# Last feed-forward group of an encoder trunk in seven products, and two gate products side by side

## The chip, the cores and the metric

The kernel runs on 1 core of one Trainium2 chip. The time is device microseconds (us) of one execution of the whole program. The engines in the tables are PE (matmul; PEld is its weight load), DVE (vector), ACT (scalar, activation), POOL (here: the issuer of accumulating DMAs) and SP (the issuer of the other DMAs).

## What is computed

A trunk of two layers over 768 tokens (one request of 512, one of 256) with 1024 features, everything in float32. A layer is a token mixer (attention in layer 0, a short gated convolution in layer 1), a feed-forward block with 4096 hidden features, and a gated addition of a per-layer input `p`:

```python
for i in range(DEPTH):
    h = rms_norm(x, norm_mix[i])
    x = x + (window_attention(h, ...) if i % 2 == 0 else short_conv(h, ...))
    h = rms_norm(x, norm_mlp[i])
    x = x + jnp.square(jax.nn.relu(h @ mlp_w_up[i])) @ mlp_w_down[i]
    gate = jax.nn.sigmoid(rms_norm(x, norm_ple[i]) @ ple_w_gate[i])
    x = x + (p[i] @ ple_w_proj[i]) * gate
return rms_norm(x, final_norm)
```

The change touches the end of the feed-forward block and the start of the gate, in both layers.

## The kernel before

`x` lies transposed: 8 blocks of 128 features by 768 tokens. Every float32 matrix product is made of three products of split operands: high weight by high input, high by low, low by high. The high part is a rounded copy (ACT, "hi"), the low part is the source minus the high part (DVE, "lo", 128x1024 for one block of weights; or a DMA that adds the source onto the negated high part, issued by POOL: `added`, tiles `vlo`).

Most of the feed-forward block uses a scheme of seven products where four times two halves would take eight: the weights of two blocks are read as a 2x2 grid and give w11, w12, w22 and the sums s1 to s4; the inputs give x11, x21, x22 and the sums t1 to t4 (class `Acts`). `product7` is one such product, over half of the tokens (H = 384 columns), accumulated in a PSUM bank. ACT copies intermediate banks into other banks (`C` and `B` from `a`, `p` from `b`), and later products accumulate into the copies.

`mlp(l, ...)` runs 16 units `up` (each makes 128-row blocks of the hidden features; its results are `y1`, `y2`) and, for each group g of two units, `down` in two halves h (4 of the 8 blocks of `x` each, 14 products of 6 matmuls). The body stands in `manual_schedule`: on ACT, PE and DVE the instructions run in the order in which the code is written, and each engine takes them strictly in that order. In a half of `down` the order on PE is w11, s3, s2, w12, s1, w22, s4. Between them DVE adds the finished banks to `x` (lines 1341 and 1363) and, for the step after, prepares the weight sums (lines 419 to 425) and low parts (line 464); ACT makes the copies (1336, 1357) and the high parts (444).

The last group, g = 7, is different: `last_down` makes it with plain products (`group2`, line 131), 4 chunks of 48 matmuls of 384 columns. After each two blocks of `x`, `add` (line 869) brings the result into `x`, and `nxt.block` makes the high part (ACT, 188), the low part (DVE, 189) and the square (ACT 198, DVE 199) of that block for the norm ahead of the gates.

The gates follow: eight products of 48 matmuls, one for each block of gate columns (512-column and 256-column pieces of tokens apart in layer 1). `ple` is layer 0: after the first gate product come the four `ss` matmuls (the sum of squares) and the chain to `rstd` (the norm's factor); each gate then is multiplied with `rstd` (DVE, 1463), goes through the sigmoid (ACT, 1466), is multiplied with the projected `p` (1469) and added to `x` (1470), and the block is prepared for layer 1's mixer. Its products 0 to 5 are ordered by the framework, the others by hand. `last_ple` is layer 1: first all weights, then two gate products, then `rstd`.

Of the kernel before, what the change touches and what calls it, by code (L numbers as in the profile page):

```python
# [11 lines left out]
F32 = mybir.dt.float32  # L12
F32R = mybir.dt.float32r
# [5 lines left out]
P = 128  # L19
# [28 lines left out]
def trunk_kernel(ctx: ExitStack, tc: tile.TileContext, a: dict, out: bass.AP):  # L48
# [124 lines left out]
    class Norm:  # L173
# [4 lines left out]
        def __init__(self, i, name, places, acc, rstd=None):  # L178
            self.i, self.name, self.places, self.rplace = i, name, places, rstd
            self.xs = [], []  # L180
            self.acc = slot(acc, f"acc_{name}", F32)[:, : self.n]

        def block(self, m, xb):
            g = gain(self.i, m)
            hi, lo = (slot(self.places[8 * p + m], f"xs_{self.name}") for p in range(2))
            self.xs[0].append(hi[:])
            self.xs[1].append(lo[:])
            act.activation(hi[:], xb, AF.Copy, scale=g)
            dve.scalar_tensor_tensor(lo[:], xb, g, hi[:].bitcast(F32), ALU.mult, ALU.subtract)
            self.square(m, xb)  # L190
# [854 lines left out]
    def mlp(l, norm, nxt, w, places, early, product=None, begun=None):  # L1045
# [14 lines left out]
        def acts_of(u, y1, y2, rest):  # L1060

            own = places[7 * (u % 2) : 7 * (u % 2) + 7]
            e = Acts(y1, y2, own, groups[u // 2], u % 2)
            if u < 2 * NG - 2:
                return [
                    lambda: squared(rest),
                    lambda: e.highx(0),
                    lambda: (e.highx(1), e.lowx(0), e.lowx(1), e.t13()),
                    e.t42,
                    lambda: e.high(0),  # L1070
                    lambda: e.high(1),
                    lambda: e.low(0),
                    lambda: e.low(1),
                ]

            def whole(i, q):
                hi, lo = slot(own[2 * i], "act"), slot(own[2 * i + 1], "act")
                split(hi[:], lo[:], q[:])
                groups[u // 2].setdefault("whole", {})[u % 2, i] = hi[:], lo[:]

            return [lambda: squared(rest), lambda: whole(1, y2), lambda: whole(0, y1)]
# [22 lines left out]
        def up_begun(u, w, make, then):  # L1104
# [71 lines left out]
        def up_plain(u, w, make, then):  # L1176
# [91 lines left out]
        def up(u, w, make, then):  # L1268


            first = u == PLAIN[l]
# [35 lines left out]
            rectified(y1, c, 0, H, ALU.max)  # L1307
            late()
            if seven:
                v.low("direct")  # L1310
            else:
                v = [then(0)]
# [5 lines left out]
            squared(y2)  # L1318
            product7(a, w, "s4", xs, False)
            rectified(y1, a, H, T, ALU.max)  # L1320
            pend.extend(acts_of(u, y1, y2, y1))
            return v

        def down(g, h, w, make, then):

            xg = groups[g]
            top, low = ([x(4 * h + 2 * i + s) for s in range(2)] for i in range(2))
# [14 lines left out]

            w.low("s32")
# [9 lines left out]
            b = [bank("B", "b")[:, :H] for _ in range(2)]  # L1353
            products(b, "s3", True)
            p = big("p")
            for i in range(2):
                act.activation(p[:, i * H : i * H + H], b[i], AF.Copy)
            products(a, "s2", False)
            d = copies("B", a)
            for i in range(2):  # L1360
                t = low[i].rearrange("p (a n) -> p a n", a=2)
                q = p[:, None, i * H : i * H + H].broadcast_to([P, 2, H])
                dve.tensor_tensor(t, t, q, ALU.subtract)
# [15 lines left out]
        def last_down(chunks, then):  # L1379
            late(9)  # L1380
            src = [groups[NG - 1]["whole"][k] for k in ((0, 0), (1, 0), (0, 1), (1, 1))]
            for j in range(KB // 2):
                if j + 1 < KB // 2:
                    chunks.append(then(j + 1))
                ps = [both(), both()]
                ts = [terms_of(chunks[j], [[t[p] for t in src] for p in range(2)], col=i * P) for i in range(2)]

                for i, part in ((0, 0), (1, 0), (0, 1), (1, 1)) if j == 0 else ((0, None), (1, None)):
                    if part is None:
                        group2(ps[i], ts[i])  # L1390
                    else:
                        group2(ps[i], (ts[i][::2], ts[i][:0:-2])[part], part == 0, part == 1)
                    if part != 0:
                        m = 2 * j + i
                        add(m, ps[i])
                        nxt.block(m, x(m))
# [5 lines left out]
        for g in range(NG - 1):  # L1402
            jobs += [ups[2 * g + 2], (down, g, 0), (down, g, 1), ups[2 * g + 3]]
        with tc.manual_schedule(engines={ET.Activation, ET.PE, ET.DVE}):
            for i, (job, *args) in enumerate(jobs):

                def make():

                    if i + 1 == len(jobs):
                        return None  # L1410
                    what, *n = jobs[i + 1]
                    if what is not down:
                        return up_chunk(l, *n)
                    k = (KB // 2) * n[0] + 2 * n[1]
                    return Weights7(a_down[k], a_down[k + 1])

                a_down = a["down"][l]
                w = job(*args, w, make, lambda j: weight(a["down"][l, (NG - 1) * (KB // 2) + j], FG))
            last_down(w, lambda j: weight(a["down"][l, (NG - 1) * (KB // 2) + j], FG))
# [24 lines left out]
    def ple(norm, nxt):  # L1444
# [30 lines left out]
        for i in range(5):  # L1475
            gp = product(PAIRED[i], weights(i))
# [59 lines left out]
    def last_ple(norm, full, rest, prs, ys, finals):  # L1536

        rest = [[slot(rest[2 * p + i], "gwr") for i in range(2)] for p in range(2)]
        ws = []
        for m in range(KB):  # L1540
            if m < 2:
                w = weight(a["gate"][1, m], KB)
            else:
                raw, i = fetch(a["gate"][1, m]), m - 2
                most = [slot(full[6 * p + i], "gw")[:] for p in range(2)]
                less = [rest[p][i // 3][:, i % 3 * (CH - T) : (i % 3 + 1) * (CH - T)] for p in range(2)]
                split(*most, raw[:, :T])
                split(*less, raw[:, T:])
                w = tuple(blocks(most[p], T // P) + blocks(less[p], (CH - T) // P) for p in range(2))
            ws.append(w)  # L1550
# [9 lines left out]
        gps = [product(first, m) for m in range(2)]  # L1560
# [10 lines left out]
        outs = [more.tile([P, CH], F32, tag=tag, name="o", bufs=1) for tag in ("sum0", "sum1", "zhi", "zlo")]  # L1571
# [30 lines left out]
        def stored(n):  # L1602

            for _ in range(n):
                i = left.pop(0)
                o = outs[i // 2][:, i % 2 * s0 : i % 2 * s0 + s0]
# [282 lines left out]
    with tc.manual_schedule(engines={ET.Activation, ET.PE, ET.DVE}):  # L1889
        w0, *begun = first_tail(n1, act0[5:7] + act0[12:], *head)  # L1890
        mlp(0, n1, n2, w0, act0, KB // 2, begun=begun)
    n3 = Norm7(1, "mix1", xs3, aside3, rest[24], spare=dict(zip(("ah", "al", "v"), old[13:])))
    wc = ple(n2, n3)
# [4 lines left out]
    mlp(1, n4, n5, w1, act1, KB // 2, begun=begun)  # L1898
    last_ple(
        n5,  # L1900
        full=xs1[17:] + act1[:1],
        rest=act1[1:5],
        prs=act1[5:8],
        ys=act1[8:11],
        finals=((act1[11], act1[12]), (act1[13], xs1[16])),
# [79 lines left out]
```

## Time and profile before

| | before |
|---|---|
| median of 3 runs | 1660.08 us (1659.68 to 1662.16) |
| the profiled execution | 1661.51 us, its span 1659.5 us |
| mean granted clock of TensorE | 0.996 |
| busy PE / DVE / ACT / POOL | 1637.6 / 1380.8 / 948.5 / 71.7 us |
| layer 0: group 6's two halves, `last_down`, first gate begins | at 705.64, 749.77 and 783.15 us |
| layer 1: `last_down`, first gate begins | at 1543.07 and 1576.59 us |

A line of the timeline has the start (us), the duration of the first instruction to the last one of the row, the engine, the line of the program, the operation, output<-input tiles, shapes and the number of instructions; brackets hold the idle time ahead of it and what ended that. A window's line has the window's length, busy time and count of each engine, the granted clock, the DMA share and GB/s. A line of waits has the engine and instruction, what it waited for, the sum, how often, and the longest.

### The profile page before, as it was taken

What the parts mean: (1) busy time and instruction counts of PE and PEld (TensorE: products, weight loads), DVE (VectorE), ACT (ScalarE), POOL (GpSimd) and SP (SyncE); (2) the same over time, 40 slices, a digit from 0 to 9 for tenths busy, and PEclk for the clock granted to TensorE, in tenths of its full rate; (3) what the DMA queues carried; (4) which work ended last, traced back from release to release, by engine and by line L of the source; (5) the groups of instructions that cost most, each with busy time, mean ns of one, the idle gap of its engine ahead of it and who ended that gap; (6) DMA issues with size and microseconds to landing.
All of it is one profiled execution on the core that took longest, in us unless ns stands there. A gap on an engine that the chain in (4) does not pass through costs nothing.

```text
span 1659.5 us, 24297 instructions
## 1 busy us (share of the span) xinstructions
PE 1637.6 (99%) x9414; PEld 1587.3 (96%) x9414; DVE 1380.8 (83%) x2242; ACT 948.5 (57%) x1508; POOL 71.7 (4%) x104
## 2 busy tenths in 40 slices
PE   8999999999999999999999999999999999999997
PEld 7988789999999999999999999999999999999986
DVE  7598888898889889877888777778889888988776
ACT  7377766865556556545654434555555655655554
POOL 0211000000000000000000000000000000000000
PEclk9999999999999999999999999999999999999998
DMA  8755322443233333242312222112333323333222
GB/s 267 199 154 149 87 64 83 121 109 87 83 86 96 96 96 91 71 122 69 98 62 77 76 77 76 64 64 73 87 96 96 95 87 79 90 96 108 69 87 99
DMA packets 55476, 161.11 MB, mean 97 GB/s; under 512 B 7056, under 2 KB 10128, under 8 KB 55360
## 3 DMA queue, kind: packets, MB, share of 16 engines
q1 hardware_dynamic: 45184, 139.89, 26.4%
q0 software_dynamic: 10176, 19.67, 6.7%
q8 instruction: 74, 1.21, 0.3%
q14 instruction: 42, 0.34, 0.1%
HBM read 138.82 MB, written 10.48 MB: 90 GB/s over the span
## 4 chain that ended last, share of the span: by engine, by line
PE 88%; DVE 7%; ACT 4%; issue 1%; DMA 0%; DVEq 0%; SPq 0%; ACTq 0%
PE a L486 33%; PE mm L131 10%; PE mm L140 8%; PE b L486 8%; PE d L486 5%; PE c L486 5%; PE B L486 4%; PE C L486 4%; PE gate L140 3%; PE pt L760 1%; PE p L1096 1%; PE p L1199 1%; PE gate L131 1%; PE O L770 1%; PE O L771 1%
## 5 line engine op out<-in xcount | busy, mean ns | idle before, releaser
L486 PE MATMUL a<-xs,whi 128*128 128x384 f32 x624 | 121.8, 337 | 0.0
L444 ACT ACTIVATE vhi<-wraw 128x512 fp32r<-128x512 f32 x67 | 42.2, 631 | 132.3 <-PE B L486 87.9
L486 PEld LDWEIGHTS a<-xs,whi 128*128 128x128 f32 x624 | 110.0, 188 | 0.2 <-DVE y L1306 0.2
L486 PE MATMUL a<-t,zhi 128*128 128x384 f32 x536 | 109.1, 337 | 0.0
L486 PE MATMUL a<-t,whi 128*128 128x384 f32 x536 | 108.8, 336 | 0.0
L486 PE MATMUL b<-t,zhi 128*128 128x384 f32 x536 | 108.7, 336 | 0.0
L1341 DVE TENSOR_TENSOR x<-x,a 128x384 f32<-128x384 f32 x112 | 62.1, 554 | 55.3 <-PE a L486 55.3
L486 PE MATMUL a<-act,whi 128*128 128x384 f32 x448 | 96.5, 337 | 0.0
L486 PEld LDWEIGHTS a<-t,whi 128*128 128x128 f32 x536 | 94.9, 188 | 0.0
L486 PEld LDWEIGHTS b<-t,zhi 128*128 128x128 f32 x536 | 94.9, 188 | 0.0
L486 PEld LDWEIGHTS a<-t,zhi 128*128 128x128 f32 x536 | 94.8, 188 | 0.0
L464 DVE TENSOR_TENSOR wlo<-wraw,whi 128x1024 fp32r<-128x1024 f32 x70 | 85.2, 1218 | 7.9 <-ACT whi L444 7.9
L444 ACT ACTIVATE whi<-sum 128x1024 fp32r<-128x1024 f32 x67 | 70.6, 1054 | 27.0 <-PE a L486 22.7
L464 DVE TENSOR_TENSOR wlo<-sum,whi 128x1024 fp32r<-128x1024 f32 x67 | 81.8, 1220 | 5.1 <-ACT whi L444 5.1
L1058 ACT ACTIVATE y<-y 128x768 f32<-128x768 f32 x64 | 53.7, 839 | 54.4 <-DVE y L1055 54.3
L464 DVE TENSOR_TENSOR zlo<-sum,zhi 128x1024 fp32r<-128x1024 f32 x67 | 81.5, 1217 | 0.0
L140 PE MATMUL mm<-xs_mix,whi 128*128 128x512 f32 (+1 forms) x320 | 81.0, 341 | 0.0
L486 PEld LDWEIGHTS a<-act,whi 128*128 128x128 f32 x448 | 79.8, 188 | 0.0
L444 ACT ACTIVATE whi<-wraw 128x1024 fp32r<-128x1024 f32 x72 | 75.7, 1051 | 7.0 <-PE C L486 7.0
L444 ACT ACTIVATE zhi<-sum 128x1024 fp32r<-128x1024 f32 x67 | 70.9, 1058 | 11.9 <-DVE sum L420 11.0
L486 PE MATMUL a<-xs,wlo 128*128 128x384 f32 x312 | 67.1, 336 | 0.0
L358 ACT ACTIVATE t<-y 128x768 fp32r<-128x768 f32 x56 | 45.7, 838 | 34.9 <-DVE y L349 34.4
(345 smaller groups left out, 4558.4 us busy)
## 6 DMA issues: line engine op xcount, KB each, us to landing
wraw<-in_up SPq DMA_DIRECT2D x64, 512.0 KB, 3.9
wraw<-in_down SPq DMA_DIRECT2D x64, 512.0 KB, 4.2
wraw<-in_w_in SPq DMA_DIRECT2D x24, 512.0 KB, 3.5
wraw<-in_gate SPq DMA_DIRECT2D x16, 512.0 KB, 3.4
vlo<-in_up POOLq DMA_DIRECT2D x28, 256.0 KB, 5.6
vlo<-in_down POOLq DMA_DIRECT2D x28, 256.0 KB, 6.0
pj<-pjs SPq DMA_DIRECT2D x16, 384.0 KB, 2.8
wraw<-in_w_q SPq DMA_DIRECT2D x8, 512.0 KB, 4.6
```

The costliest lines, as they stand in the source:

```text
L131: pe.matmul(t, lhsT=w, rhs=x[:, o:e], start=first and i == 0 and j == 0, stop=last and i == n - 1 and j == 2)
L140: pe.matmul(ps[:, o:e], lhsT=w, rhs=x[:, o:e], start=i == 0 and j == 0, stop=i == n - 1 and j == 2,)
L358: act.activation(t[0][:], (self.q1, self.q2)[i][:], AF.Copy)
L444: act.activation(hi[:], src, AF.Copy)
L464: dve.tensor_tensor(lo[:], src, hi[:].bitcast(F32), ALU.subtract)
L486: pe.matmul(ps, lhsT=a, rhs=b, start=start and i == 0, stop=i == len(terms) - 1, skip_group_check=True)
L760: pe.transpose(pt[:, h * P : (h + 1) * P], lg[h // 2][:, h % 2, b * P : (b + 1) * P], ident[:],)
L770: pe.matmul(O[:], lhsT=v, rhs=ph[:], start=b == 0, stop=False)
L771: pe.matmul(O[:], lhsT=v, rhs=pl[:], start=False, stop=b == nk - 1)
L1058: act.activation(t[:], t[:], AF.Square)
L1096: pe.matmul(ps[o], lhsT=wt[:, c], rhs=xs[f"x{h + 1}{1 + o}"][m][part], start=k == 0 and j == 0, stop=k == KB - 1 and j == 2,)
L1341: dve.tensor_tensor(t[:, o : o + H], t[:, o : o + H], f, op)
```

## The change

1. The last group's `down` becomes seven products in two halves as well, in functions of their own: `down_first` and `down_last`. The order on PE in them is w11, w12, s3, s2, s1, w22, s4. The last unit's `y1` and `y2` are squared and split inside `up` (`final`) and `down_first`. The preparation of the `x` blocks for the gates stands between the products of `down_last`.
2. `Norm.block` is split into `high`, `low` and `square`.
3. The first two gate products of a layer run side by side, in three stretches of blocks (2,3,0,1, then 6,7, then 4,5), ahead of the sum of squares (`first_gates`). Their weights are made in `down_last`; the first one's low part comes by `weight_added`: two ACT copies and an accumulating DMA of 512 KB.
4. `ple` and `last_ple` take these two products (`gps`) and begin with the norm's factor.

```diff
+    def weight_added(src):
+        raw = fetch(src)
+        hi, lo = (wp.tile([P, CH], F32R, name=f"w{p}", bufs=2) for p in ("hi", "lo"))
+        act.activation(hi[:], raw[:], AF.Copy)
+        act.activation(lo[:], hi[:].bitcast(F32), AF.Copy, scale=-1.0)
+        nc.gpsimd.dma_start(lo[:], src, accum_op=ALU.add)
+        return blocks(hi[:], KB), blocks(lo[:], KB)
+
+    def first_gates(norm, ws, n):
...
+        gps = [both("gate") if n == T else [fresh("gate")[:, :n]] for _ in ws]
+        order = 2, 3, 0, 1, 6, 7, 4, 5
+        for ks in (order[:4], order[4:6], order[6:]):
+            for gp, (hi, lo) in zip(gps, ws):
+                for k in ks:
+                    for j, (wt, part) in enumerate(((hi, 0), (hi, 1), (lo, 0))):
...
         def up(u, w, make):
...
             rectified(y1, c, 0, H, ALU.max)
+            if final:
+                e = chunk_acts(u, y1, y2)
+                act.activation(y1[:, :H], y1[:, :H], AF.Square)
+                e.highx(0)
...
             squared(y2)
+            if final:
+                e.highx(1)
+                v.low("s32")
             product7(a, w, "s4", xs, False)
...
+        def down_first(w, make, top, low, products, copies, added, third, less):
+            e = aside.pop()
+            a = [bank("A", "a")[:, :H] for _ in range(2)]
+            products(a, "w11", True)
+            e.lowx(1)
+            act.activation(e.q1[:, H:], e.q1[:, H:], AF.Square)
+            c = copies("C", a)
+            e.t13()
+            e.high(0)
+            e.t42()
+            products(c, "w12", False)
+            e.low(0)
+            e.high(1)
+            p = third()
+            e.low(1)
+            w.split("s14")
+            added(top, 0, c, ALU.add)
+            products(a, "s2", False)
+            d = copies("B", a)
+            v = make()
+            v.sums32()
+            v.sums14()
+            v.high("s32")
+            less(p)
+            products(a, "s1", False)
+            v.high("direct")
+            added(low, H, a, ALU.subtract)
+            v.low("direct")
+            products(d, "w22", False)
+            v.added("w22")
+            added(low, 0, d, ALU.subtract)
+            products(a, "s4", False)
+            return v, lambda: added(top, H, a, ALU.add)
+
+        def down_last(w, before, top, low, products, copies, added, third, less):
+            src = [a["gate"][l, PAIRED[m] if l == 0 else m] for m in range(2)]
+            ws = []
+            w.low("s32")
+            w.split("s14")
+            before()
+            t = [bank("A", "a")[:, :H] for _ in range(2)]
+            products(t, "w11", True)
+            for m in (2, 3):
+                nxt.high(m, x(m))
+                nxt.low(m, x(m))
+            c = copies("C", t)
+            products(c, "w12", False)
+            for m in (0, 1):
+                nxt.high(m, x(m))
+                nxt.low(m, x(m))
+            added(top, 0, c, ALU.add)
+            p = third()
+            ws.append(weight_added(src[0]))
+            products(t, "s2", False)
+            d = copies("B", t)
+            less(p)
+            for m in (2, 3):
+                nxt.square(m, x(m))
+            ws.append(weight(src[1], KB, tag="z"))
+            products(t, "s1", False)
+            added(low, H, t, ALU.subtract)
+            for m in (0, 1):
+                nxt.square(m, x(m))
+            products(d, "w22", False)
+            added(low, 0, d, ALU.subtract)
+            products(t, "s4", False)
...
-        def last_down(chunks, then):
...
-            last_down(w, lambda j: weight(a["down"][l, (NG - 1) * (KB // 2) + j], FG))
+            return w, first_gates(nxt, w, (T, SEQS[0])[l])
...
         for i in range(5):
-            gp = product(PAIRED[i], weights(i))
+            gp = gps[i] if i < 2 else product(PAIRED[i], weights(i))
             r = norm.rstd(psum) if r is None else r
```

Three places where the order of instructions changes. The first is DVE where PE runs the first half of the last group (layer 0). Before, in `last_down`: `act` are the low parts of the hidden features, `mm` the finished banks, `xs_ple` the low parts for the gates.

```order
L85 TENSOR_TENSOR act<-y_7951,act 128x768
L85 TENSOR_TENSOR act<-y_7950,act 128x768
L85 TENSOR_TENSOR wlo<-wraw,whi 128x1024
L869 TENSOR_TENSOR x<-x,mm 128x384 x2
L189 SCALAR_TENSOR_TENSOR xs_ple_8046<-x,vec,xs_ple_8045 128x768
L869 TENSOR_TENSOR x<-x,mm 128x384 x2
```

And now, in `down_first`, from the low part of s1 and s4 to the first reading of `a`:

```order
L469 TENSOR_TENSOR wlo<-sum,whi 128x1024
L1353 TENSOR_TENSOR x<-x,C 128x384 x2
L424 TENSOR_TENSOR sum<-wraw 128x512
L425 TENSOR_TENSOR sum<-sum,wraw 128x512
L429 TENSOR_TENSOR sum<-wraw 128x512
L430 TENSOR_TENSOR sum<-wraw,sum 128x512
L1367 TENSOR_TENSOR x<-x,p 128x768 x2
L1353 TENSOR_TENSOR x<-x,a 128x384 x2
```

The low part, four additions of weights and the subtraction of `p` now stand between the third product and the reading of `a`, on which s4 (it writes `a` anew) depends.

The second is ACT in the last half. Before, in `last_down`, where only weights and blocks for the gates were made:

```order
L84 ACTIVATE whi<-wraw 128x1024
L188 ACTIVATE xs_ple_8045<-x,vec 128x768
L195 ACTIVATE acc_ple_3332<-x 128x768
L188 ACTIVATE xs_ple_8064<-x,vec 128x768
L198 ACTIVATE sq<-x 128x768
L84 ACTIVATE whi<-wraw 128x1024
```

And now, in `down_last` (`C`, `B`, `p` are the copies of banks; L1507 and L1508 are the first gate's weights):

```order
L449 ACTIVATE whi<-sum 128x1024
L186 ACTIVATE xs_ple_8191<-x,vec 128x768
L186 ACTIVATE xs_ple_8195<-x,vec 128x768
L1348 ACTIVATE C<-a 128x384 x2
L186 ACTIVATE xs_ple_8215<-x,vec 128x768
L186 ACTIVATE xs_ple_8219<-x,vec 128x768
L1360 ACTIVATE p<-b 128x384 x2
L1507 ACTIVATE whi<-wraw 128x1024
L1508 ACTIVATE wlo<-whi 128x1024
L1348 ACTIVATE B<-a 128x384 x2
```

The copies for which PE waits (`C` ahead of w12, `B` ahead of s1) stand behind blocks and weights for the gates.

The third is DVE in layer 0's `ple`, around the low part of the sixth gate's weights (`wlo`). Before:

```order
L1463 TENSOR_TENSOR gt<-gate,rstd_ple_8373 128x384 x2
L348 TENSOR_TENSOR q<-q 128x384
L85 TENSOR_TENSOR wlo<-wraw,whi 128x1024
L1469 TENSOR_TENSOR gt<-pr,gt 128x768
L1470 TENSOR_TENSOR x<-x,gt 128x768
```

There `gate` in the first row is the fourth gate. Now:

```order
L1585 TENSOR_TENSOR gt<-gate,rstd_ple_8477 128x384
L1591 TENSOR_TENSOR gt<-pr,gt 128x768
L1585 TENSOR_TENSOR gt<-gate,rstd_ple_8477 128x384
L1592 TENSOR_TENSOR x<-x,gt 128x768
L85 TENSOR_TENSOR wlo<-wraw,whi 128x1024
```

Here `gate` is the fifth one, and the product and the addition between are the fourth's: the same weights stand one gate later on DVE. In the whole program PE has 48 instructions fewer, DVE 50 more, ACT 48 more, POOL 6 more, and SP as many as before.

190 lines of the change are left out of this document (106 added, 84 removed).

## The prediction

> **What bounds the kernel now.** I read the page's busy time, granted clock and chain first.
>
> ```profile
> PE 1637.6 (99%) x9414; PEld 1587.3 (96%) x9414; DVE 1380.8 (83%) x2242; ACT 948.5 (57%) x1508; POOL 71.7 (4%) x104
> ...
> PEclk9999999999999999999999999999999999999998
> ...
> PE 88%; DVE 7%; ACT 4%; issue 1%; DMA 0%; DVEq 0%; SPq 0%; ACTq 0%
> ```
>
> PE is busy for 99% of the span at full clock and carries 88% of the chain, so a matmul taken away is worth its own time, and a wait put into PE costs its own length. Next come PE's waits (total, times, longest) and PE's load in three stretches (length; busy PE, PEld, DVE, ACT, POOL; clock; DMA share, GB/s): group 6's two halves of `down`, then `last_down` of each layer.
>
> ```profile
> PE mm L140 <- ACT p0h L84: 6.1, 1, 6.1
> ...
> PE b L486 <- DVE zlo L464: 0.4, 1, 0.4
> ```
> ```profile
> 705.64:735.05 29.41, 29.41 (x169) 29.41 (x169) 24.26 (x35) 15.81 (x25) 1.52 (x3) 1.00 0.35 96
> 750.00:783.00 33.00, 33.00 (x192) 33.00 (x191) 24.40 (x33) 18.03 (x22) 0.00 (x0) 1.00 0.21 73
> 1543.30:1576.60 33.30, 33.30 (x193) 33.30 (x192) 25.68 (x35) 19.48 (x25) 0.00 (x0) 1.00 0.25 80
> ```
>
> The 6.1 us is the start of the program; no wait lies in the last groups. All three stretches are full on PE, with DVE at 82%, 74% and 77%: there is nothing to gain but matmuls, and DVE has about 5 us of room in a pair of halves.
>
> **What is removed.** PE's timeline gives the starts.
>
> ```profile
> 705.64 0.86 PE L486 MATMUL a<-act,whi 128*128 128x384 f32 x4
> ...
> 735.05 1.57 PE L486 MATMUL a<-xs,whi 128*128 128x384 f32 x8
> ...
> 749.77 0.86 PE L131 MATMUL mm<-act,whi 128*128 128x384 f32 x4
> ...
> 783.15 0.86 PE L131 MATMUL gate<-xs_ple,whi 128*128 128x384 f32 x4
> ```
>
> Two seven-product halves: 735.05 − 705.64 = 29.41 us (168 matmuls; one product of 12 takes 2.10). `last_down`: 783.15 − 749.77 = 33.38 us (192 matmuls). So 3.97 us of PE go away in each layer, 7.94 in all. The two gates hold as many matmuls as before, whatever their order: nothing.
>
> **What is put in.** The bodies are in a fixed order and each engine takes its own strictly, so I add up what stands ahead of each thing PE waits for. The old halves give the prices, from start to start where a queue is full.
>
> ```profile
> 709.11 0.69 DVE L419 TENSOR_TENSOR sum<-wraw 128x512 f32<-128x512 f32 x1
> 709.83 0.69 DVE L420 TENSOR_TENSOR sum<-sum,wraw 128x512 f32<-128x512 f32 x1
> 710.44 1.82 DVE L1363 TENSOR_TENSOR x<-x,p 128x768 f32<-128x768 f32 x2
> 712.18 0.69 DVE L424 TENSOR_TENSOR sum<-wraw 128x512 f32<-128x512 f32 x1
> 712.78 0.68 DVE L425 TENSOR_TENSOR sum<-wraw,sum 128x512 f32<-128x512 f32 x1
> 713.38 0.55 DVE L1341 TENSOR_TENSOR x<-x,C 128x384 f32<-128x384 f32 x1
> ...
> 722.15 1.22 DVE L464 TENSOR_TENSOR wlo<-sum,whi 128x1024 fp32r<-128x1024 f32 x1
> 723.29 0.69 DVE L419 TENSOR_TENSOR sum<-wraw 128x512 f32<-128x512 f32 x1
> ...
> 732.63 1.06 DVE L1341 TENSOR_TENSOR x<-x,B 128x384 f32<-128x384 f32 x2
> ...
> 735.25 0.56 DVE L1341 TENSOR_TENSOR x<-x,a 128x384 f32<-128x384 f32 x1 [0.51 <-PE a L486]
> ```
> ```profile
> 706.88 1.05 ACT L444 ACTIVATE whi<-sum 128x1024 fp32r<-128x1024 f32 x1
> 707.84 0.83 ACT L1058 ACTIVATE y<-y 128x768 f32<-128x768 f32 x1
> 708.57 0.84 ACT L1336 ACTIVATE C<-a 128x384 f32<-128x384 f32 x2
> ...
> 710.02 0.49 ACT L1357 ACTIVATE p<-b 128x384 f32<-128x384 f32 x1 [0.20 <-PE b L486]
> ...
> 757.11 0.94 ACT L188 ACTIVATE xs_ple<-x,vec 128x768 fp32r<-128x768 f32 x1 [3.29 <-DVE x L869]
> ```
>
> From the start of PE's next product (735.05) to the first instruction on the last one's result (735.25) pass 0.20 us.
>
> *First half, s1 and s4.* Both hang on DVE's list behind s3: 0.20, the copy `p` 0.49, `whi` 1.05 (in old halves it stands ahead of the copies, at 706.88; now behind `p`), its `wlo` 1.14 (722.15 to 723.29), two `C` additions 1.06, the four sums 0.72 + 0.61 + 0.60 + 0.60, `x` less `p` 1.73 (710.44 to 712.18, rounded), and reading `a` 0.56: 8.76. PE has s2, s1, w22 until s4: 3 × 2.10 = 6.30. In the old order w12 also stood there (8.40). So PE waits about 2.5 (0.3 of it ahead of s1's low part).
>
> *Second half, w12.* It needs `C`. ACT's `whi` of s1/s4 has to wait for the first half's s4 to leave the buffer: 0.20 + 0.96 + two blocks for the gates at about 0.84 each (0.94 at 757.11, less the 0.1 that two neighbours overlap) + 0.47 for a copy = 3.3, against w11's 2.10: 1.2.
>
> *Second half, s1.* It needs `B`, which now stands behind the gate's `whi` and `wlo`: 0.20 + 0.41 + 0.96 + 0.96 + 0.47 = 3.0, against s2's 2.10: 0.9.
>
> *Smaller ones.* First half's w12: from the end of the last unit's w22, `lo` of x11 (0.6 left), the last part of `y2` 0.56, its minimum 0.96, then ACT's square and high part 0.85 each, half a square 0.49, `C` 0.47, with 0.20: 5.0 against s4 and w11, 4.20: 0.8. First half's s3: from the high part of x2 on, DVE has a low part 0.87, four sums of half a block for t1 to t4 at 0.56 (priced as the row at 735.25) and another low part 0.87: 4.0; meanwhile pass half a square and `C` on ACT (0.9), w12 and three matmuls of s3 (2.6): 0.5. Second half's s4: ACT's rest of the copies 0.2, two squares 1.5, the second gate's `zhi` 1.05, then `zlo` 1.22 and reading `a` 0.56: 4.5 against s1 and w22, 4.20: 0.3.
>
> What a restart costs stands where PE waits now:
>
> ```profile
> 354.13 1.22 DVE L464 TENSOR_TENSOR zlo<-sum,zhi 128x1024 fp32r<-128x1024 f32 x1
> ...
> 355.39 0.30 PEld L486 LDWEIGHTS b<-t,zlo 128*128 128x128 f32 x2 [0.70 <-DVE zlo L464]
> ```
>
> 0.04 us after DVE, the weight load starts with the wait's end rather than ahead of it, and costs about 0.1 more. [...]
>
> Sum of a layer: 2.5 + 1.2 + 0.9 + 0.8 + 0.5 + 0.3 + seven restarts 0.7 = 6.9, less 3.97: **+2.9**. The waits' lower end is 0, as in the old halves (29.41 us, full); I take the sum, since it prices the new lists, not the old, and its upper end a fifth above, 8.3, where each link also pays the 0.04 us and more that an engine needs to see another's end. Layer 1's halves are the same code: +5.9 for both.
>
> The first gate's low part comes by DMA instead of DVE.
>
> ```profile
> wlo<-in_up POOLq DMA_DIRECT2D x2, 512.0 KB, 6.1
> ```
>
> 6.1 us from issue to landing. The negated copy is done 0.20 + 0.41 + 0.96 + 1.06 = 2.6 us after the second half's s3; until the gates PE has s2, s1, w22 and s4, 8.4, with 1.4 of waits: 7.2 us are there. It just fits: 0, at worst 1 a layer if POOL or its queue adds more than that. SP issues as many transfers as before: 0. DVE's and ACT's other new work lies under PE.
>
> *Layer 0's gates.* The factor used to be ready 14.0 us after the first gate began (797.16 − 783.15); now its sum stands behind two gates of 8.35 us instead of one, so it comes at about 22.4, and DVE starts on the gates 8 us late, with more waiting for it.
>
> ```profile
> 796.20 0.96 DVE L270 SCALAR_TENSOR_TENSOR rstd_ple<-v,y 128x768 f32<-128x768 f32 x1
> ...
> 800.63 0.56 DVE L1463 TENSOR_TENSOR gt<-gate,rstd_ple 128x384 f32<-128x384 f32 x1 [0.54 <-PE gate L131]
> 801.10 0.95 DVE L1470 TENSOR_TENSOR x<-x,gt 128x768 f32<-128x768 f32 x1
> 801.97 0.55 DVE L1463 TENSOR_TENSOR gt<-gate,rstd_ple 128x384 f32<-128x384 f32 x1
> ...
> 820.10 1.22 DVE L85 TENSOR_TENSOR wlo<-wraw,whi 128x1024 fp32r<-128x1024 f32 x1
> ```
>
> The sixth gate's `wlo` was made at 820.10, 4.4 us before its gate (five products of 8.35 and the sums after 783.15, at 825.7). Now DVE first waits for the fifth gate's end: 0.20, two multiplications by the factor 0.47 each with the fourth gate's product and addition 0.87 each between, `wlo` 1.22: 4.1. PE has 8 matmuls of high parts to do, 1.4. It waits 2.7, with the restart **+2.8**; from 0 (if DVE gets that far ahead) to 5 (if the seventh and eighth gates wait too). In layer 1 all weights stand ahead of the factor: 0.
>
> Altogether +5.9 + 2.8 = +8.7: the profiled execution would go from 1661.51 to 1670.2; it lay 1.43 above the median of the runs, so the median goes from 1660.08 to **1668.8**.
>
> **Rivals.** *The halves keep PE full as the old ones do, and the gates too*: 1660.08 − 7.9 = 1652.1. For it: 29.41 us without a gap at the same load. It is decided at the first half's s4: if DVE's list between s3 and the reading of `a` takes under 6.3 us, that wait goes, and with it most of what follows. Against it: the prices above are of the same instructions in a full queue. 0.13. *Only the two longest waits of a layer last*: 2 × (2.5 + 1.2 + 0.2 − 3.97) ≈ 0, no wait in the gates: 1660. 0.08. *The gates' wait is hidden*, as DVE overtakes before the fifth gate: 1666. 0.15. *The clock.* PE's first matmuls come after 6 us without any:
>
> ```profile
> 6.00:12.00 6.00, 5.93 (x19) 4.41 (x20) 3.83 (x4) 3.56 (x6) 0.00 (x0) 1.00 1.00 389
> 12.00:18.00 6.00, 6.00 (x37) 5.21 (x36) 4.66 (x6) 5.57 (x8) 0.00 (x0) 1.00 1.04 392
> ```
>
> 19 matmuls in the first 6 us, 37 in the next: a restart that went like this would lose 6 × 18/37 = 2.9 us (the record shows clock 1.00 in both, and weights also arrive there). My longest waits, 2.3 and 2.8, are less than half of that pause. If the three of them did so: 1668.8 + 3 × 2.9 = 1677.5; 0.06. [...]
>
> **Numbers.** The forecast itself has 0.58, with its own range 1664 to 1673. A measurement here can tell 0.2%, 3.3 us: same is 1656.8 to 1663.4. Faster: 0.13 and a quarter of the even case, 0.15; same: half of it and the edge of the forecast, 0.07; slower 0.78. From 1659 to 1675 the range leaves out the fast rival and the clock.
>
> **What would show it.** In the profile after: PE 48 instructions shorter, the chain with more of DVE and ACT; in the view of PE's waits, `a` on DVE's `x` (about 2.3, twice), `C` and `a` on ACT's copies (about 1 each, six times), the gate on `wlo` (2.8, once); in windows the last group at about 36 us instead of 33.4. I am wrong if those waits are absent, or if PE's waits shift to a stage that this sum leaves out, such as the first gate on its DMA.

## The result and the profile after

The changed kernel took 1673.2 us (median of 6 runs, 1671.13 to 1673.83) against 1661.1 (6 runs, 1659.68 to 1662.77): the ratio is 1.0071, with an interval of 1.0058 to 1.0084. It is 12.1 us slower, where 8.7 were predicted. The profiled execution took 1673.83 us, its span 1671.9 (before: 1659.5), so the spans differ by 12.4.

The page's busy time and its chain by engine:

```profile
PE 1638.1 (98%) x9366; PEld 1581.6 (95%) x9366; DVE 1413.4 (85%) x2292; ACT 974.4 (58%) x1556; POOL 77.0 (5%) x110
...
PE 83%; DVE 9%; ACT 6%; issue 1%; DMA 1%; DVEq 0%; SPq 0%; ACTq 0%
```

PE has its 48 matmuls less. At the price of a full queue that is 8 us, yet it is busy for as long as before, so the others must have taken longer: 174.9 ns each on the mean (1638.1 us for 9366), where it was 174.0 before. DVE and ACT have 4% more of the chain between them. PE's waits (total, times, longest):

```profile
PE mm L140 <- ACT p0h L84: 6.0, 1, 6.0
PE a L491 <- DVE x L1353: 3.8, 2, 1.9
PE C L491 <- ACT C L1348: 2.2, 4, 0.7
PE a L491 <- ACT B L1348: 1.8, 2, 0.9
PE gate L131 <- DVE wlo L85: 1.8, 1, 1.8
...
PE b L491 <- DVE t L369: 0.9, 2, 0.4
PE ss L243 <- ACT ah L84: 0.7, 1, 0.7
```

The start of the program is as before. The next four rows and the one of `t` are new: the last group now waits for DVE's `x` once a layer, for a copy three times, for `t` once. This is how PE's timeline shows the longest wait of layer 0's halves, s4 of the first one, which is twelve matmuls, and w11 behind it:

```profile
765.37 1.46 PE L491 MATMUL a<-act,whi 128*128 128x384 f32 x4 [1.89 <-DVE x L1353]
766.62 0.84 PE L491 MATMUL a<-act,wlo 128*128 128x384 f32 x2
767.26 1.49 PE L491 MATMUL a<-act,whi 128*128 128x384 f32 x4
768.54 0.74 PE L491 MATMUL a<-act,wlo 128*128 128x384 f32 x2
769.12 0.86 PE L491 MATMUL a<-act,whi 128*128 128x384 f32 x4
```

Read the starts, not only the bracket: from 765.37 to 769.12 the product takes 3.75 us, where 2.10 is the price in a full queue. Two matmuls are 0.64 us apart (766.62 to 767.26), 0.320 for one, against 0.35 for two, 0.174 for one, elsewhere. The windows of the same stretch (length; busy PE, PEld, DVE, ACT, POOL; clock; DMA share, GB/s):

```profile
763.00:765.30 2.30, 0.48 (x3) 0.16 (x1) 2.30 (x5) 2.10 (x4) 0.00 (x0) 1.00 0.00 0
765.30:768.00 2.70, 2.63 (x9) 2.63 (x10) 2.70 (x6) 0.00 (x0) 0.90 (x1) 0.56 0.87 224
...
833.80:837.40 3.60, 3.60 (x13) 3.60 (x13) 3.60 (x6) 1.02 (x2) 0.00 (x0) 0.53 0.53 170
837.40:841.00 3.60, 3.60 (x23) 3.60 (x22) 3.60 (x6) 2.67 (x4) 0.00 (x0) 1.00 0.31 92
```

PE waits in the first window, at clock 1.00, and works in the second at a granted clock of 0.56. The same comes behind the wait of the sixth gate: 13 matmuls in 3.6 us at 0.53, then 23 in 3.6 us at 1.00. I call this a dip of the clock. The profile after has three of them that before did not have: behind s4 in layer 0, behind s4 in layer 1 (0.60 there, from 1567.20 to 1569.90) and in layer 0's gates. The kernel before has one of its own, in layer 0's attention, which this execution of the change has not:

```profile
202.24:205.65 3.41, 3.17 (x9) 2.59 (x10) 3.41 (x12) 1.97 (x7) 0.00 (x0) 0.50 0.39 152
```

Where the 12.4 us lie, from the starts of the stages in the two profiled executions: layer 0's last group 37.23 for 33.38 us (+3.85), its gates up to the mixer's first products 71.93 for 67.66 (+4.27), layer 1's last group 37.11 for 33.52 (+3.59), all that follows there 84.05 for 82.91 (+1.14), the stretch from layer 0's end to layer 1's last group +0.44, all ahead of the first last group −0.89 (the dip at 202.24 lies there).

### The profile page after: what moved, and what is told of

The parts are those of the page before. It is cut to its first block, busy times and chain, and to the rows that moved or that the text cites. A ratio compares the mean times of both kernels' runs of the same rounds, so it can differ in the third digit from the quotient of the medians.

```text
span 1671.9 us, 24321 instructions
## 1 busy us (share of the span) xinstructions
PE 1638.1 (98%) x9366; PEld 1581.6 (95%) x9366; DVE 1413.4 (85%) x2292; ACT 974.4 (58%) x1556; POOL 77.0 (5%) x110
## 4 chain that ended last, share of the span: by engine, by line
PE 83%; DVE 9%; ACT 6%; issue 1%; DMA 1%; DVEq 0%; SPq 0%; ACTq 0%
PE a L491 32%; PE b L491 8%; PE mm L140 8%; PE mm L131 5%; PE c L491 5%; PE d L491 4%; PE C L491 4%; PE B L491 4%; PE gate L140 2%; PE gate L131 1%; PE pt L765 1%; PE gate L1526 1%; PE p L1095 1%; PE p L1198 1%; PE O L775 1%
## 5 line engine op out<-in xcount | busy, mean ns | idle before, releaser
L491 PE MATMUL a<-t,whi 128*128 128x384 f32 x568 | 116.0, 337 | 1.8 <-ACT B L1348 1.8
L491 PE MATMUL b<-t,zhi 128*128 128x384 f32 x568 | 116.1, 336 | 0.9 <-DVE t L369 0.9
L1353 DVE TENSOR_TENSOR x<-x,a 128x384 f32<-128x384 f32 x128 | 70.2, 554 | 55.3 <-PE a L491 55.3
L491 PE MATMUL a<-act,whi 128*128 128x384 f32 x512 | 112.9, 343 | 3.9 <-DVE x L1353 3.8
L491 PE MATMUL a<-t,zhi 128*128 128x384 f32 x568 | 116.0, 337 | 0.0
L491 PEld LDWEIGHTS a<-t,whi 128*128 128x128 f32 x568 | 100.3, 188 | 2.7 <-ACT B L1348 2.4
L491 PEld LDWEIGHTS b<-t,zhi 128*128 128x128 f32 x568 | 100.5, 188 | 1.5 <-DVE t L369 1.5
L491 PEld LDWEIGHTS a<-t,zhi 128*128 128x128 f32 x568 | 100.5, 188 | 0.0
L491 PEld LDWEIGHTS a<-act,whi 128*128 128x128 f32 x512 | 92.9, 191 | 5.2 <-DVE x L1353 5.2
L363 ACT ACTIVATE t<-y 128x768 fp32r<-128x768 f32 x64 | 52.5, 839 | 42.9 <-DVE y L354 41.6
```

What stands on the lines that cost most here:

```text
L363: act.activation(t[0][:], (self.q1, self.q2)[i][:], AF.Copy)
L491: pe.matmul(ps, lhsT=a, rhs=b, start=start and i == 0, stop=i == len(terms) - 1, skip_group_check=True)
L1353: dve.tensor_tensor(t[:, o : o + H], t[:, o : o + H], f, op)
```

## The experiments

Each run is compared with runs of the kernel before on the same chip.

### Which things of the halves are late

The first experiment takes the sums of weights out of DVE's list ahead of the reading of `a` on which s4 waits:

```diff
             v = make()
-            v.sums32()
-            v.sums14()
-            v.high("s32")
             less(p)
             products(a, "s1", False)
             v.high("direct")
             added(low, H, a, ALU.subtract)
             v.low("direct")
+            v.sums32()
             products(d, "w22", False)
             v.added("w22")
+            v.high("s32")
             added(low, 0, d, ALU.subtract)
+            v.sums14()
             products(a, "s4", False)
```

> The changed kernel, with the four sums of weights in the first half moved behind the reading of a (2.53 us of DVE less between s3 and that reading). Theory A (PE waits for the written order, and after a wait of about 1.9 us the granted clock halves for some 3.3 us): DVE's list falls from 8.4 to about 5.9 us, under PE's 6.3, so the wait of 1.9 us goes in both layers, and with it the slow stretch of 1.6 us behind it: about 7 us less than the changed kernel, 1666. Theory B (the slow stretch behind the wait is not from the wait but from what runs there, the accumulating DMA and the copies): the wait of 1.9 goes, the slow stretch stays: 3.8 us less, 1669.5. Theory C (something later on DVE comes last instead): under 2 us less.

It took 1674.64 us (4 runs), ratio 1.0080 (1.0065 to 1.0095): not better than the change itself. The wait of 1.9 us is gone in both layers, and w12 of the second half waits longer. First PE's waits and its timeline, then ACT's timeline there:

```profile
PE C L491 <- ACT C L1348: 8.1, 4, 3.4
...
772.79 0.96 PE L491 MATMUL C<-act,whi 128*128 128x384 f32 x4 [3.41 <-ACT C L1348]
```
```profile
769.66 1.06 ACT L449 ACTIVATE whi<-sum 128x1024 fp32r<-128x1024 f32 x1 [1.13 <-DVE sum L430]
770.62 1.75 ACT L186 ACTIVATE xs_ple<-x,vec 128x768 fp32r<-128x768 f32 x2
772.27 0.84 ACT L1348 ACTIVATE C<-a 128x384 f32<-128x384 f32 x2
```

The copy `C` is short and its input long there. It stands in ACT's list behind the high part of a sum of weights, which now comes from DVE late, and behind two blocks for the gates. The sums had only been moved from one wait to the next, and a dip followed the 3.41 too (four matmuls from 774.14 to 775.42 us, 0.32 each).

The second experiment leaves the sums and brings the copies forward in the second half:

```diff
+            c = copies("C", t)
             for m in (2, 3):
                 nxt.high(m, x(m))
                 nxt.low(m, x(m))
-            c = copies("C", t)
...
             p = third()
-            ws.append(weight_added(src[0]))
             products(t, "s2", False)
             d = copies("B", t)
+            ws.append(weight_added(src[0]))
```

> The changed kernel, with the second half's C copies ahead of two blocks for the gates on ACT, and its B copies ahead of the first gate's weights. Theory A: the waits ahead of w12 (0.55 and 0.35) and s1 (0.9 each) go: about 2.7 us less in two layers, 1670.5; if the first gate's low part now lands too late (its DMA is issued about 1 us later), up to 2 of that comes back. Theory B (ACT's copies are late for another reason): no change.

1675.85 us (4 runs), ratio 1.0092 (1.0075 to 1.0109). PE's waits:

```profile
PE a L491 <- DVE x L1353: 9.2, 4, 2.8
...
PE gate L1526 <- DMA wlo<-in_gate: 1.8, 1, 1.8
```

The waits of w12 and s1 behind the second half's copies are gone. What ACT makes for DVE is later instead, and s4 of the second half now waits 2.62 and 2.77 us for DVE. The low part of the first gate, which is asked for later, lands 1.77 us too late in layer 1.

The third one arranges both halves anew: the first as in the first experiment; in the second, copies come first, the blocks of `x` are prepared one to three products later, the first gate's weight is asked for at once behind the first block, and the squares go to the end. The gates are those of the change.

```diff
             products(t, "w11", True)
-            for m in (2, 3):
-                nxt.high(m, x(m))
-                nxt.low(m, x(m))
             c = copies("C", t)
+            w.split("s14")
+            before()
             products(c, "w12", False)
+            nxt.high(2, x(2))
+            nxt.low(2, x(2))
+            ws.append(weight_added(src[0]))
             added(top, 0, c, ALU.add)
             p = third()
             products(t, "s2", False)
             d = copies("B", t)
             less(p)
+            nxt.high(3, x(3))
+            nxt.low(3, x(3))
             products(t, "s1", False)
...
```

> The changed kernel, with both halves of the last group in another order on ACT and DVE, and nothing else: in the first the sums of weights behind the reading of a; in the second the C copies first, then the s1/s4 weights, one block, the first gate's weights as soon as w12 has left their buffer, p, B, and the other blocks and squares behind them; the reading of a ahead of the gate's low weights. Theory A (only the order makes PE wait; there is room for all of it): of the seven waits of a layer only those of the first half at w12 and s3 (0.6 and 0.4) stay, the last group takes about 31 us instead of 37.2: 1673.2 - 2 x 6 = 1661. Theory B (DVE and ACT have too much work in the last group, so every order moves the wait): a new wait of 1 to 3 us a layer shows up, and the time stays above 1667.

1661.26 us (10 runs) against 1660.01, ratio 1.0001 (0.9992 to 1.0011). The last group in one window of layer 0, from its w11 to the first gate, and PE's waits:

```profile
751.32:782.59 31.27, 30.24 (x170) 29.25 (x170) 27.77 (x41) 22.55 (x34) 2.48 (x3) 1.00 0.49 137
```
```profile
PE gate L131 <- DVE wlo L85: 1.8, 1, 1.8
...
PE C L491 <- ACT C L1348: 1.3, 2, 0.7
...
PE b L491 <- DVE t L369: 0.8, 2, 0.4
```

The last group takes 31.27 and 31.41 us, 2.1 less than before in each layer and 5.8 less than in the change, with two waits left in it and no dip. Twice 5.8 are 11.6 us, and the ratios 1.0071 and 1.0001 differ by 0.7%, 11.6 us. So another order of the two halves wins back about as much as the change had lost, and the seven products themselves bring some 4 us. The gates, 4.3 us longer than before, use them up: 71.91 us, as in the change.

### What sets off a dip

The kernel before, with one edit: DVE is held up by additional subtractions in the second half of 14 groups, by 1.4 to 5.3 us, so that PE has pauses of different lengths at the same place of the code.

```diff
             products(a, "s1", False)
+            if h:
+                late_by = 1.4 + 0.3 * (2 * g + l)
+                while late_by > 0.2:
+                    n = min(768, int((late_by - 0.07) / 0.00104) // 16 * 16)
+                    dve.tensor_tensor(p[:, :n], p[:, :n], p[:, :n], ALU.subtract)
+                    late_by -= 0.07 + n * 0.00104
             added(low, H, a, ALU.subtract)
```

> The kernel before, with DVE held up by 1.4 to 5.3 us, in steps of 0.3, ahead of the reading of a in the second half of 14 groups (extra subtractions on a tile that nobody reads any more), so that PE waits from 0 to about 3.7 us. Theory A (a pause from somewhere between 0.9 and 1.9 us on halves the clock for about 3.3 us, at a price of about 1.6 us whatever its length): the short pauses are followed by matmuls of 174 ns, those from a bound on by some 10 at twice that. [...] Theory C (it depends on when the pause falls in a free-running window): pauses of 1.5 to 3 us are followed by a slow stretch in some places and not in others.

One run, 1677.47 us. PE has nine pauses, 13.4 us in all, the longest 2.52 us in layer 0 and 2.75 in layer 1. No dip follows any of them. The timeline and the window behind the longest:

```profile
1542.67 0.97 PE L486 MATMUL a<-act,whi 128*128 128x384 f32 x4 [2.75 <-DVE x L1341]
...
1542.67:1545.70 3.03, 3.02 (x17) 3.03 (x18) 3.03 (x6) 0.97 (x2) 0.00 (x0) 1.00 0.75 139
```

By this run alone the dips would have nothing to do with the pauses. But it has each length once. The next run has few lengths many times: the same edit without `if h:`, 4.5 us in layer 0 and 5.4 in layer 1.

> The kernel before, with DVE held up by 4.5 us (layer 0) and 5.4 us (layer 1) ahead of the reading of a in every half of the 14 groups, so that PE pauses at many places for about 1.9 and 2.8 us, twice in 15 us. Theory A (a single pause of 1.9 us is enough): slow stretches behind all of them. Theory C (it depends on when the pause falls): slow stretches behind some of them, more at 2.8 than at 1.9 us; none at 2.8, after none behind the five single pauses of 1.2 to 2.8, would speak for a sum of several pauses in a short time as the cause.

One run, 1751.77 us, mean granted clock 0.983. PE has 28 pauses of two lengths. The same product at another pause of 2.75 us, with its window:

```profile
1527.58 1.65 PE L486 MATMUL a<-act,whi 128*128 128x384 f32 x4 [2.75 <-DVE x L1341]
1529.03 0.84 PE L486 MATMUL a<-act,wlo 128*128 128x384 f32 x2
...
1527.58:1531.00 3.42, 3.42 (x11) 3.42 (x12) 2.94 (x5) 0.00 (x0) 0.00 (x0) 0.50 0.87 152
```

Compare 11 matmuls in 3.42 us here with 17 in 3.03 behind the equal pause above. Of 14 pauses of about 1.74 us three are followed by a dip, of 14 of about 2.75 us seven. What decides is not the length alone: equal pauses of the same instruction in one execution differ. That fits Theory C of the expectation, by which it depends on when the pause falls.

The traces also record when the granted clock changes, and this bears the theory out. In the change the dips begin at 765.62, 833.88 and 1567.75 us, 20 and 215 multiples of 3.413 us apart, and each lasts 3.41 us; behind the pauses they last 3.41 us or twice that. If the time of each run is cut into stretches of this length, counted from where its recorded clock changes, the two pauses of 2.75 us above look as follows: first the one with the dip, then the one without.

```profile
1523.40:1526.81 3.41, 1.43 (x9) 1.11 (x7) 3.31 (x4) 1.26 (x2) 0.59 (x1) 1.00 0.19 41
1526.81:1530.23 3.42, 2.65 (x8) 2.65 (x9) 3.42 (x7) 0.00 (x0) 0.31 (x1) 0.50 0.86 195
1530.23:1533.64 3.41, 3.41 (x12) 3.41 (x12) 2.10 (x4) 1.06 (x1) 0.00 (x0) 0.50 0.49 148
...
1537.81:1541.22 3.41, 2.11 (x13) 1.79 (x11) 3.27 (x5) 1.26 (x2) 0.00 (x0) 1.00 0.00 0
1541.22:1544.64 3.42, 1.97 (x11) 1.97 (x12) 3.42 (x6) 0.00 (x0) 0.89 (x1) 1.00 0.77 194
```

A stretch less PE's busy time is PE's idle time. In the first case 1.98 us of the pause lie in one stretch, and the dip begins with the next one; in the second the border divides the pause into 1.30 and 1.45 us, and there is no dip. Of the 14 pauses of about 2.75 us, the seven with 1.93 us or more in one stretch are followed by a dip, the seven with at most 1.85 are not. Of the pauses of 1.74 us, nine have at least 1.69 in one stretch, and the three dips are among them; the other five are divided further and have none. So between 1.69 and 1.85 us both occur, and what decides there is open. Idle time is not all of it either: the dip of the kernel before at 202.24 us follows a stretch with 1.3 us idle (PE busy for 2.10 of the 3.41 us from 198.83).

A dip of one stretch costs about 1.5 us: 1.65 at s4 of layer 0's first half in the change (3.75 less 2.10), and 1.56 by estimate from 3.41 us at 0.320 instead of 0.174 us for a matmul. Four of the seven behind the longer pauses last two stretches; in these the pause runs on into the second one by 0.71 to 0.82 us.

### What becomes of the wait in layer 0's gates

The change, with the sum of squares moved 3 us ahead, in front of the last block of the first gate:

```diff
-            for gp, (hi, lo) in zip(gps, ws):
+            for gi, (gp, (hi, lo)) in enumerate(zip(gps, ws)):
                 for k in ks:
+                    if gi == 0 and k == order[7] and n == T:
+                        ss = norm.sum_squares(psum)
```

> The changed kernel, with layer 0's sum of squares 18 matmuls before the end of the first gate's last stretch, not behind both gates (about 3.1 us earlier); the framework then places the sixth gate's low weights ahead of the fifth gate's end on DVE. Theory A: the waits of 0.35 and 1.77 us in the gates and the slow stretch behind them (1.5) go, so about 3.7 us less, 1669.5. Theory B (the gates' loss is from the order of blocks or the side by side, not from the late factor): no change, 1673.

1670.81 us (4 runs), ratio 1.0052 (1.0037 to 1.0067). The sixth gate's wait is gone. The eighth waits instead: 1.39 us for its high part and 0.41 for its low part, again with a dip (four matmuls from 849.38 to 850.66 us, 0.32 each). That the run is 2.4 us shorter than the change cannot be put down to the edit, since in its profile the halves have no dips, behind the same waits of 1.9 us (at most 1.43 us of the one in layer 0 lie in one stretch, 1.82 of the one in layer 1). The window stands where the change had 0.56:

```profile
767.03 0.96 PE L491 MATMUL a<-act,whi 128*128 128x384 f32 x4 [1.90 <-DVE x L1353]
...
767.00:769.70 2.70, 2.67 (x15) 2.67 (x16) 2.70 (x5) 0.63 (x1) 0.90 (x1) 1.00 0.86 228
```

Next, the factor as late as in the change, but the weights of each gate asked for one gate earlier:

```diff
+        ws = {2: weights(2)}
-        for i in range(5):
-            gp = gps[i] if i < 2 else product(PAIRED[i], weights(i))
+        for i in range(6):
+            gp = gps[i] if i < 2 else product(PAIRED[i], ws.pop(i))
+            if 2 <= i + 1 < 6 and i + 1 not in ws:
+                ws[i + 1] = weights(i + 1)
...
-            for step in steps(5, gp):
-                step()
+            times, sigmoid, added, block = steps(5, gp)
+            times()
             w7 = weights(7)
+            sigmoid()
+            added()
+            block()
```

> The changed kernel, with the factor as late as it is, but the weights of each next gate asked for ahead of the steps of the gate before (and the eighth gate's between the multiplication and the sigmoid of the sixth), so that the framework puts the sixth gate's low weights ahead of the fifth gate's end on DVE. Theory A (the wait in the gates is the place of that one low part in DVE's list): the waits of 0.35 and 1.77 us and the slow stretch of 1.5 behind them go, none comes in their place: about 3.5 us less, 1669.7. Theory B (DVE, 8 us late, has too much to do until the gates end, whatever the order): the wait comes back at a later gate, under 1.5 us gained.

1671.87 us (4 runs), ratio 1.0074 (1.0059 to 1.0089). No gate waits any more, and the mixer's first products do, by 2.25 us, with a dip (866.88, 867.20, 867.52 us: 0.32 for one):

```profile
PE c L1897 <- ACT xs L317: 2.2, 1, 2.2
```

Three further kernels combine the rearranged halves, the earlier sum of squares and the earlier weights, and then move more of layer 0's end forward, one thing behind the other. The first is the sum of these edits:

> The orders of both halves, the earlier sum of squares in layer 0 and the earlier gate weights together. Theory A: 7.9 us of matmuls gone, waits of about 1.2 us a layer in the first half and about 1 us at the end left: 1661.3 - 7.9 + 2 x 1.2 + 1 = 1657, faster than the kernel before by 0.25%. Theory B: the waits come back in other places, and the time is not below 1661.

1660.87 us (10 runs) against 1660.01, ratio 1.0003 (0.9994 to 1.0013). The gates take 68.09 us, but `c` waits 2.63 us at the mixer's start, with a dip (862.19, 862.51, 862.83 us: 0.32 for one). The next one puts the eighth gate's multiplication, sigmoid and addition ahead of the preparation of the seventh block:

```diff
             gp = product(PAIRED[7], w7)
             c.high("direct")
             times()
             c.low("direct")
             sigmoid()
             c.high("second")
             added()
             sums.high(0)
+            times, sigmoid, added7, _ = steps(7, gp)
+            times()
+            c.low("second")
+            sigmoid()
+            added7()
             block()
```

> As the last combination, and in layer 0 the eighth gate's multiplication, sigmoid and addition ahead of the seventh block's and the sums' preparation on DVE and ACT, since there the last 2.6 us of the factor's lateness came out. Theory A: this wait goes too, with the slow stretch behind it (1.4), and nothing else is late: 1660.9 - 4 = 1657, faster than the kernel before by 0.2 to 0.3%. Theory B (the lateness is DVE's work and not its order): the wait shows up behind the gates in the first products of the mixer, and the time is not below 1660.

1660.2 us (11 runs) against 1659.81, ratio 0.9997 (0.9988 to 1.0006). `c` no longer waits, the mixer's sum of squares does, 1.5 us. The last one brings the eighth block's square and its part of the sum forward:

```diff
             nxt.plain_block(m, x(m))
+            sq = big("sq")
+            act.activation(sq[:], x(m), AF.Square)
+            nxt.last = nxt.gated
+            nxt.table()
+            dve.tensor_tensor(nxt.acc, nxt.acc, sq[:], ALU.add)
+            parts = nxt.acc_parts()
             sums.high(1)
```

> As the last one, and the eighth block's square and the parts of its sum ahead of the sums' preparation, since there PE waited 1.46 and 0.55 us ahead of the mixer's sum of squares, with a slow stretch of about 1 behind it. Theory A: 1660.2 - 3 = 1657, below the kernel before by 0.15 to 0.2%. Theory B (what DVE is late by shows up once more behind it): the first products of the mixer's seven wait for their t sums instead, and the time stays at 1660.

1661.32 us (11 runs) against 1660.04, ratio 1.0004 (0.9995 to 1.0013). PE's row of waits and the timeline at the place:

```profile
PE b L491 <- DVE v L262: 3.1, 1, 3.1
...
870.41 2.93 PE L491 MATMUL b<-t,zhi 128*128 128x384 f32 x8 [3.11 <-DVE v L262]
873.13 1.49 PE L491 MATMUL b<-t,zlo 128*128 128x384 f32 x4
874.41 1.80 PE L491 MATMUL a<-t,zhi 128*128 128x384 f32 x5
```

The sum of squares has no wait left, and the first product behind it has one of 3.11, with the matmuls at 0.32 us (873.13 to 874.41 for four). From the change to this kernel PE met the wait at the sixth gate, the eighth, at `c`, at the sum of squares and behind it. That reads as work of DVE that is late in this part, where an order only chooses at which place PE meets it: in the change DVE is busy for 46.45 of the 49.79 us from the factor to the mixer's first products (before: 47.95 of 53.65). No run here takes work from DVE, so this is argued and not shown. In the change DVE can begin on the gates 8 us later than before, because the factor does: its last step stands in DVE's timeline of the change at

```profile
807.29 0.96 DVE L275 SCALAR_TENSOR_TENSOR rstd_ple<-v,y 128x768 f32<-128x768 f32 x1
```

that is, ready 22.1 us after the first gate's start at 786.11, and 14.0 before. No version tried here beats the kernel before by more than the measurement can tell.

## Why the prediction was right, and where it was not

**Sign and kind.** The slots whose lists were added up are the ones that wait, each for the engine and tile named. The price of two full halves, 29.41 us, holds to within 0.9 us: the rearranged ones have 1.0 us of waits and take 31.27.

**The waits of a layer's halves**, predicted and then measured in layer 0:

| place | predicted | measured |
|---|---|---|
| first half, s4 (with s1's low part) | 2.5 | 1.89 + 0.24 |
| second half, w12 on `C` | 1.2 | 0.55 |
| second half, s1 on `B` | 0.9 | 0.91 |
| first half, w12 on `C` | 0.8 | 0.63 |
| first half, s3 on `t` | 0.5 | 0.44 |
| second half, s4 | 0.3 | 0.1 |
| sum | 6.2 | 4.8 |

The sum is 1.4 us too high, above all at w12 of the second half: 3.3 us were counted from s4's end to the copy, and 2.8 passed from the start of w11 (769.12) to that of w12 (771.92).

**The step that failed is the price of a pause.** It was put at its own length and 0.1 us for a restart, and the clock rival was set aside because the longest waits, 2.3 and 2.8 us, are less than half of the 6 us at the program's start. The runs showed that a pause of 1.74 us can be enough (3 of 14). Layer 0's last group took 37.23 us against 29.41 for two full halves, 7.8 more: 4.8 of waits, 1.65 for the dip (3.75 less 2.10) and 1.4 left for the seven restarts and what the records don't resolve, 0.2 each rather than 0.1. So 7.8 instead of 6.9, in which smaller waits and the dip partly cancel.

That a restart costs something at all could not be read from the prediction's row at 355.39: it loads `zlo`, the very weights that PE waited for. The profile after shows it. Here the weights were ready, PE waited for a bank, and the load still begins only with the end of the wait:

```profile
765.37 0.95 PEld L491 LDWEIGHTS a<-act,whi 128*128 128x128 f32 x4 [2.21 <-DVE x L1353]
```

**The clock rival** was right in part. There were three dips at the three places it named, but with matmuls slower by 1.5 to 1.65 us each, not 2.9, and by where the pause fell rather than always. A dip can also cost less than that. The profiles with the earlier sum of squares and with the earlier weights have no dips in the halves: layer 0's last group takes 35.84 and 35.89 us there against 37.23, so its dip cost 1.4; layer 1's takes 37.12 and 36.73 against 37.11, so there the dip cost at most 0.4. That dips come in one run and not in another shows in the granted clock of the change's runs too: it was 0.997 in the shortest (1671.13 us) and 0.994 or 0.995 in the other five (1672.47 to 1673.83).

**Layer 0's gates.** The wait for `wlo` was put at 2.7, and was 0.35 for the high part and 1.77 for the low part, 2.1. With the dip behind it, 1.5, the stage lost 4.27 instead of 2.8. The factor's lateness was 8.1 us, as worked out.

**What was priced at nothing.** The DMA of the first gate's low part fitted, as said. The second experiment shows how closely: asked for one product later, it came 1.77 us late in layer 1. Layer 1's end lost 1.14 us where 0 was taken: the first gate waits 0.30 for a block, and the sum of squares 0.66 for ACT's `ah`, neither of which was in the sum.

Layer 1's halves were taken as the same code, and on ACT they are not quite: weights of later gates (`gw`) stand between the blocks there, and one has to land first. The profile with the earlier sum of squares shows it free of a dip, on ACT and then on PE:

```profile
1573.17 0.85 ACT L84 ACTIVATE gw<-wraw 128x768 fp32r<-128x768 f32 x1 [2.31 <-DMA wraw<-in_gate]
...
1579.20 0.96 PE L491 MATMUL a<-t,whi 128*128 128x384 f32 x4 [2.09 <-ACT B L1348]
```

PE waits 2.09 us for `B` where 0.9 was counted. In the change, where the dip had already made PE late, it waits 0.89: one delay stands in for the other.

**The rival of full halves** needed DVE's list behind s3 to be under 6.3 us. In the change as written it was not. The rearranged kernel shows that the same products with hardly a wait do exist, so this was a property of the order, not of the seven products.

## What to carry to other kernels

In engines that take a fixed list strictly, add up the list ahead of each thing the bound engine waits for: that named the waits of layer 0's halves and gates here, and gave their sum within a third, single ones less well. An edit that removes one wait by moving work on one engine is to be followed to the next thing that this work, or what now stands behind it, delivers: twice here the wait came back longer at a later product. By these runs a pause of 2 us in PE is to be priced at its length plus a share of 1.5 us for the clock, by how likely it is to lie mostly in one stretch of 3.41 us (seven of 14 pauses of 2.75 us were followed by a dip, three of 14 of 1.74), so a saving of 4 us that brings three such pauses is gone.

## What the hardware showed unexpectedly

The clock fell to about half behind pauses of 1.7 to 2.8 us, in 3 of 14 cases at 1.74 us and in 7 of 14 at 2.75, for 3.41 us or twice that, with 0.320 us for a matmul of 384 columns instead of 0.174. Equal pauses had no effect elsewhere in the same execution. Where the pause lay against stretches of 3.413 us, at whose borders the recorded clock changes, told the two kinds of the 2.75 us pauses apart. The rows at 765.37 (1.89 us of wait, then a granted clock of 0.56) and 1527.58 (2.75, then 0.50) show such pauses with a dip, the one at 1542.67 (2.75, then 1.00) one without.
